# A planner that knows of the SBUF port which VectorE and GpSimd share

## The chip, the cores and the metric

The kernel runs on one core of a Trainium2 chip. The core has a matrix engine (TensorE, in the profile PE, with PEld for its weight loads), a vector engine (VectorE, DVE), an engine for activation functions (ScalarE, ACT), a general one (GpSimd, POOL) and a queue that issues DMAs (SyncE, SP). Each engine works through its own list of instructions in order and waits on semaphores for the others. The metric is device time in microseconds of one execution; shorter is better.

## What is computed

A two-layer backbone over 512 latent tokens and 256 context tokens of width 1024, all in float32. Cut to what matters:

```python
for i in range(DEPTH):                                  # 2 layers
    sh1, sc1, g1, sh2, sc2, g2 = split(silu(c) @ mod_w[i] + mod_b[i], 6)
    a = rmsnorm(h) * (1 + sc1) + sh1
    m = ab_mixer(a, ac) if i == 0 else hyena_mixer(a)   # ac: the context, modulated
    h = h + g1 * m
    u = rmsnorm(h) * (1 + sc2) + sh2
    h = h + g2 * ((silu(u @ w1) * (u @ w3)) @ w2)       # width 2816
return rmsnorm(h)
```

The first mixer runs four heads of gated DeltaNet (chunks of 64 tokens, a triangular solve per chunk, a scan in both directions) and four heads of gated linear attention. The second is a Hyena operator: a short convolution and two long convolutions, done here with DFT matrices, whose filters come from a small network of sines.

## The kernel before

The kernel is written once as a straight program, but its calls do not go to the chip directly. A `Recorder` stands in for the engines: every call becomes an `Op` with its engine, an estimated cost, its dependences and a section name, and `Recorder.schedule` then makes one order for all engines. `Recorder.issue` emits the instructions in that order, so each engine's list, and the list of DMAs on SyncE, is what the planner decided. All instructions therefore carry one line, 648, in the profile.

The planner is a list scheduler. It keeps a clock `free[e]` per engine. Again and again it takes the engine that can start first, and of the operations that are ready there by then it takes the one with the highest priority: the longest path of costs to the end, plus an offset. The offsets are the table `BOOST`: one number for a section, one for a section on one engine (`"f1@gpsimd"`), in nanoseconds of path. Sections are stages of the program: `vec`, `mlp`, `modc`, `in` (inputs and modulation), `f0` to `f3` (Hyena's filters), `g`, `n0` to `n3`, `p0` to `p3`, `i0`, `i2`, `s0` to `s3`, `l0`, `l1`, `h0` to `h3`, `z0` to `z7` (the first mixer), `m02` to `m04`, `mods` (more modulation), `out`, `fa`, `fa0` to `fa3` with `fa0o` to `fa3o` (first feed-forward layer), `dft`, `p0h` to `p3h`, `v0h` to `v3h`, `hy`, `hyout` (Hyena), `fb` and its kin (second feed-forward layer). Some parts raise their own priority with `urgent`.

The planner also models the bank of PSUM that each matmul's output takes, ScalarE's table loads, the landing of DMAs and TensorE's clock; where TensorE would idle long it puts in a matmul on a constant tile. SBUF addresses are fixed before the planner runs and do not depend on its order.

A float32 product is made of three products of rounded numbers: `split` writes a rounded copy on ScalarE (a CAST) and the rest of it with a VectorE subtraction of two SBUF tiles (`t<-t ... fp32r`). This pair precedes nearly every matmul, for weights and for activations. GpSimd gets elementwise work on SBUF tiles: additions and subtractions in `filter_chunk`, in `gdn_scan` a scaling of 128x128 tiles, in Hyena's `conv` and `group` differences and gate products, in the feed-forward layers the weight difference `S3` of each `unit`. No GpSimd call here reads PSUM; a good part of VectorE's work does (`t<-bank,t`).

Of the kernel before, what the change touches and what calls it, by code (L numbers as in the profile page):

```python
# [19 lines left out]
P = 128  # L20
# [12 lines left out]
BOOST = {"": 1200, "@gpsimd": 19800, "@vector": -113900, "c": -161700, "c@gpsimd": 173900, "c@sync": -82400,  # L33
         "dft": 21800, "dft@scalar": 56000, "dft@sync": 21800, "dft@vector": -318200, "end": 12900,
         "end@scalar": -111300, "end@sync": -75800, "end@tensor": 253300, "end@vector": 46500, "f0": -3200,
# [19 lines left out]
         "fb@scalar": 22200, "fb@tensor": -4600, "fb@vector": 7200, "ffn0": -123100, "ffn0@scalar": 54200,  # L55
# [5 lines left out]
         "h3@scalar": 117400, "h@sync": 7500, "h@tensor": -117000, "h@vector": -38300, "ht@scalar": 11900,  # L61
         "ht@tensor": 89700, "hy": -14100, "hy@scalar": 26800, "hy@sync": 111000, "hy@tensor": -100100,
         "hy@vector": -3900, "hyout": -1600, "hyout@scalar": -23500, "hyout@sync": -38900, "hyout@vector": -24700,
# [10 lines left out]
         "m15@tensor": 4100, "m15@vector": 55800, "mlp": 9500, "mlp@scalar": 51700, "mlp@sync": -11600,  # L74
         "mlp@tensor": 29000, "modc": 40000, "modc@tensor": -1400, "modc@vector": -2300, "mods": 148900,
         "mods@sync": 12100, "mods@tensor": 6000, "mods@vector": -1900, "n0": 1900, "n0@gpsimd": -6000,
# [3 lines left out]
         "out@scalar": -2900, "out@sync": 7000, "out@tensor": 177300, "p0": -22500, "p0@gpsimd": -483000,  # L80
# [15 lines left out]
         "vec": -17400, "vec@scalar": -72600, "vec@sync": -1400, "vec@tensor": 1000, "vec@vector": 10000,  # L96
# [131 lines left out]
class VTile:  # L228
    __slots__ = ("phys", "left", "slot", "bit", "anc")
# [3 lines left out]


class Op:
    __slots__ = ("eng", "calls", "cost", "deps", "succ", "vts", "prio", "path", "idx", "nd", "bytes", "start", "end", "ready", "sec", "tbl", "anc", "alias", "inst", "rows", "first", "last")


class EngineProxy:
# [19 lines left out]
class Recorder:  # L259
# [75 lines left out]
    def add(s, eng, name, a, k):  # L335
# [10 lines left out]
        op = None  # L346
# [2026 lines left out]
```

## Time and profile before

| | |
|---|---|
| three runs | 1673.51, 1678.25, 1680.84 us; median 1678.25 |
| the profiled execution | 1673.98 us, of which the span from first to last instruction is 1672.3 |
| TensorE busy | 1590.1 us (95%), 11356 matmuls |
| VectorE busy | 1248.1 us (75%), 2158 instructions |
| ScalarE busy | 791.1 us (47%) |
| GpSimd busy | 364.9 us (22%), 430 instructions |
| DMA | 201.25 MB, mean 120 GB/s |

Busy time is the time during which at least one instruction of the engine runs. An instruction that has started and is held up by something inside the chip counts as busy, so a long mean duration can hide a wait; the durations by shape are to be read beside the shares. A matmul's recorded end is modelled, so full busy time of TensorE is not its peak rate.

### The profile page before, as it was taken

Reading aid. Unit: us, or ns where it says so; the run is one execution under the profiler, and the core shown is the slowest. Engines: PE = TensorE matmul, PEld = TensorE weight load, DVE = VectorE, ACT = ScalarE, POOL = GpSimd, SP = SyncE. Lnnn points to the kernel's source line nnn. Section 1 sums busy time; section 2 is a strip of 40 time slices with the busy share of each in tenths; the row PEclk is TensorE's granted clock in tenths of the full one; section 3 lists DMA queues with packets and bytes.
Section 4 is the critical chain, followed back from the end, with each engine's and each line's share of the span. In section 5 each row is a group of like instructions: output and inputs, shape, how many; then the busy total and the mean of one; then the engine's idle time right before and its main releaser. Section 6 shows DMA issues by size and latency. Waiting matters only on the chain.

```text
span 1672.3 us, 29141 instructions
## 1 busy us (share of the span) xinstructions
PE 1590.1 (95%) x11356; PEld 1400.8 (84%) x11356; DVE 1248.1 (75%) x2158; ACT 791.1 (47%) x1503; POOL 364.9 (22%) x430
## 2 busy tenths in 40 slices
PE   6999889999999889999999999999999999999998
PEld 3687778778777579989989898888889898989898
DVE  4878985657375886968678688598896977868676
ACT  3556533642434444644536365343344653636353
POOL 0344653513232310101010100143440101011000
PEclk9999997998899889999999999999999999999999
DMA  8744332473266432243343354333432333333331
GB/s 284 208 146 152 108 110 68 160 234 112 75 203 211 130 114 64 82 108 90 88 125 95 109 155 134 97 108 92 133 92 76 102 89 101 99 104 98 106 96 56
DMA packets 257147, 201.25 MB, mean 120 GB/s; under 512 B 11281, under 2 KB 234447, under 8 KB 257008
## 3 DMA queue, kind: packets, MB, share of 16 engines
q1 hardware_dynamic: 257008, 199.39, 39.5%
q8 instruction: 89, 1.46, 0.4%
q14 instruction: 50, 0.41, 0.1%
HBM read 185.70 MB, written 13.66 MB: 119 GB/s over the span
## 4 chain that ended last, share of the span: by engine, by line
PE 64%; DVE 21%; ACT 5%; DMA 4%; issue 3%; POOL 3%; SPq 0%; DVEq 0%; POOLq 0%; ACTq 0%
PE bank L648 64%; DVE t L648 21%; ACT t L648 5%; POOL t L648 3%; DMA t<-in_ffn_w_dram 1%; DMA kscr<-t 0%; SPq L648 0%; DMA t<-in_mod_w_dram 0%; ACT L641 0%; DMA t<-in_dft_filt_dram 0%; DMA t<-in_hy_w_in_dram 0%; DMA t<-in_ctx_dram 0%; DMA t<-gscr 0%; DMA t<-in_hy_w_out_dram 0%; DMA t<-in_dft_fwd_dram 0%
## 5 line engine op out<-in xcount | busy, mean ns | idle before, releaser
L648 PE MATMUL bank<-t 128*128 128x256 f32 (+8 forms) x11356 | 1590.1, 316 | 76.2 <-DVE t L648 47.0
L648 PEld LDWEIGHTS bank<-t 128*128 128x128 f32 (+4 forms) x11356 | 1400.8, 183 | 265.3 <-DVE t L648 72.7
L648 DVE TENSOR_TENSOR t<-t 128x512 fp32r<-128x512 f32 (+11 forms) x1151 | 795.7, 728 | 229.3 <-ACT t L648 150.8
L648 ACT CAST t<-t 128x512 fp32r<-128x512 f32 (+4 forms) x651 | 421.6, 664 | 428.7 <-PE bank L648 203.7
L648 POOL TENSOR_TENSOR t<-t 128x256 f32<-128x256 f32 (+3 forms) x230 | 268.5, 1186 | 952.2 <-DMA t<-in_ffn_w_dram 507.8
L648 ACT ACTIVATE t<-t 128x256 f32<-128x256 f32 (+8 forms) x314 | 156.4, 530 | 151.7 <-DVE t L648 132.0
L648 DVE TENSOR_TENSOR t<-bank,t 128x256 f32<-128x256 f32 (+5 forms) x305 | 147.3, 511 | 63.3 <-PE bank L648 50.7
L648 DVE SCALAR_TENSOR_TENSOR t<-bank,t 128x511 f32<-128x511 f32 (+4 forms) x248 | 143.1, 592 | 52.4 <-PE bank L648 35.4
L648 ACT COPY t<-bank 128x256 f32<-128x256 f32 (+2 forms) x272 | 106.8, 408 | 122.7 <-PE bank L648 119.8
L648 ACT ACTIVATE t<-bank 128x256 f32<-128x256 f32 (+7 forms) x134 | 51.0, 389 | 114.3 <-PE bank L648 111.6
L648 ACT ACTIVATE t<-bank,t 128x512 f32<-128x512 f32 (+3 forms) x94 | 51.2, 557 | 57.5 <-PE bank L648 37.4
L648 POOL COPY t<-t 32x192 f32<-32x192 f32 (+3 forms) x96 | 41.7, 440 | 132.9 <-DVE t L648 112.8
L648 DVE SCALAR_TENSOR_TENSOR t<-t 128x256 f32<-128x256 f32 (+7 forms) x134 | 59.4, 494 | 4.3 <-ACT t L648 3.8
L648 DVE SCALAR_TENSOR_TENSOR t<-t,bank 64x128 f32<-64x128 f32 (+1 forms) x112 | 38.0, 345 | 32.1 <-PE bank L648 29.5
L648 DVE COPY t<-bank 128x256 f32<-128x256 f32 (+8 forms) x70 | 31.2, 456 | 24.9 <-PE bank L648 23.4
L648 POOL TENSOR_SCALAR t<-t 128x128 f32<-128x128 f32 x40 | 31.0, 781 | 64.7 <-PE bank L648 31.5
L641 ACT ACT_TABLE_LOAD x32 | 41.1, 1283 | 1.4 <-PEq L2360 0.8
L648 POOL MEMSET t<- 32x192 f32 (+10 forms) x47 | 18.3, 394 | 78.2 <-PE bank L648 58.9
L648 DVE TENSOR_SCALAR t<-t 128x256 f32<-128x256 f32 (+5 forms) x57 | 23.9, 440 | 3.3 <-ACT t L648 2.8
L648 DVE TENSOR_TENSOR_SCAN t<-t 64x768 f32<-64x768 f32 x8 | 14.0, 1750 | 0.2
L648 DVE STREAM_TRANSPOSE t<-t 128x1024 f32<-128x1024 f32 x6 | 10.4, 1755 | 0.3
L648 POOL TENSOR_SCALAR_AFFINE_SELECT t<-t 128x512 f32<-128x512 f32 (+1 forms) x11 | 6.6, 609 | 13.2 <-DVE t L648 13.2
(15 smaller groups left out, 33.6 us busy)
## 6 DMA issues: line engine op xcount, KB each, us to landing
t<-in_mod_w_dram SPq DMA_DIRECT2D x96, 512.0 KB, 4.0
t<-in_ffn_w_dram SPq DMA_DIRECT2D x88, 512.0 KB, 4.1
t<-in_ffn_w_dram SPq DMA_DIRECT2D x48, 384.0 KB, 3.6
t<-in_ab_w_in_dram SPq DMA_DIRECT2D x28, 512.0 KB
t<-in_hy_w_in_dram SPq DMA_DIRECT2D x24, 512.0 KB, 4.3
kscr<-t SPq DMA_DIRECT2D x72, 128.0 KB, 1.8
t<-kscr SPq DMA_DIRECT2D x24, 256.0 KB, 2.6
t<-in_ffn_w_dram SPq DMA_DIRECT2D x16, 256.0 KB, 2.9
```

Source lines behind the costliest of these rows:

```text
L641: s.nc.scalar.add_instruction(mybir.InstLoadActFuncSet(name=s.nc.get_next_instruction_name(), engine=mybir.EngineType.Activation, act_func ...
L648: r = getattr(getattr(s.nc, o.eng), name)(*[b(x) for x in a], **{n: b(x) for n, x in k.items()})
```

## The change

Every instruction stays on its engine. An `Op` gets a mark `lock`. A VectorE call sets it when more than one of its inputs is a wide SBUF tile, or when it is a `tensor_copy` or `tensor_scalar` with one such input and no PSUM operand. A GpSimd call sets it unless it is a `memset`. In the planner a marked operation of one of the two engines starts no earlier than the planned end of the last marked operation of the other one (`port`). The planned start decides the order. The offsets in `BOOST` for the sections that the program uses are replaced by others, most of them, on all engines (the old and new table have some 330 entries each; those shown are a sample).

```diff
--- before.py
+++ after.py
@@ -30,77 +30,76 @@
 CH = 64
 COLS = 52480
 CW = 256
-BOOST = {"": 1200, "@gpsimd": 19800, "@vector": -113900, "c": -161700, "c@gpsimd": 173900, "c@sync": -82400,
...
+BOOST = {"": -15600, "@gpsimd": -13200, "@vector": 1000, "c": 1100, "c@gpsimd": -8600, "c@sync": 4400, "dft": 4600,
+         "f0@sync": -8700, "f0@tensor": 65300, "f0@vector": 51100, "f1": -5300, "f1@gpsimd": -142800,
+         "fa2o@tensor": -2300, "fa2o@vector": 1800, "fa3": 600, "fa3@gpsimd": 393800, "fa3@scalar": -1500,
...
@@ -233,7 +232,7 @@
 
 
 class Op:
-    __slots__ = ("eng", "calls", "cost", "deps", "succ", "vts", "prio", "path", "idx", "nd", "bytes", "start", "end", "ready", "sec", "tbl", "anc", "alias", "inst", "rows", "first", "last")
+    __slots__ = ("eng", "calls", "cost", "deps", "succ", "vts", "prio", "path", "idx", "nd", "bytes", "start", "end", "ready", "sec", "tbl", "anc", "alias", "inst", "rows", "first", "last", "lock")
 
 
 class EngineProxy:
@@ -349,7 +348,7 @@
         if op is None:
             op = Op()
             op.eng, op.calls, op.cost, op.deps, op.succ, op.vts, op.prio, op.idx = eng, [], 0.0, set(), [], {}, s.boost + BOOST.get(f"{s.sec}@{eng}", 0.0), len(s.ops)
-            op.bytes, op.tbl, op.sec, op.alias, op.inst, op.rows, op.first, op.last = 0, None, s.sec, set(), None, P, None, None
+            op.bytes, op.tbl, op.sec, op.alias, op.inst, op.rows, op.first, op.last, op.lock = 0, None, s.sec, set(), None, P, None, None, False
             s.ops.append(op)
             if s.gr is not None:
                 s.gr[0] = op
@@ -438,6 +437,8 @@
             op.last = form
             op.cost += c
         elif eng == "vector":
+            sb = sum(1 for x in ins if not isinstance(x, View) and (len(x.shape) > 2 or x.shape[1] > 1))
+            op.lock = op.lock or sb > 1 or (sb == 1 and not ps and name in ("tensor_copy", "tensor_scalar"))
             if name == "reciprocal":
                 op.cost += n * 6.25 + 68
             elif name == "tensor_tensor_scan":
@@ -452,6 +453,7 @@
             op.cost += n * 0.8333 + (51 if ps else 93) + 51 * sc
             op.tbl = k.get("func") or next((x for x in a if isinstance(x, AF)), None)
         else:
+            op.lock = name not in ("memset",)
             if name == "tensor_copy":
                 op.cost += n * 1.25 + 130
             elif name in ("memset", "affine_select"):
@@ -523,6 +525,7 @@
                 heapq.heappush(pend[o.eng], (0.0, o.prio, o.idx))
         order = []
         curtbl = form = None
+        port = {"vector": 0.0, "gpsimd": 0.0}
         low, done, placed = 0, [False] * n, 0
         left = n
         while left:
@@ -572,6 +575,9 @@
                 if g is not None and g != curtbl:
                     c += 1283
                     curtbl = g
+            if o.lock:
+                t = max(t, port["gpsimd" if e == "vector" else "vector"])
+                port[e] = t + c
             o.start, o.end = t, t + c
             if e == "tensor":
                 if form is not None and o.first != form:
@@ -627,7 +633,7 @@
         v.slot = bank
         x = s.idle
         o.eng, o.calls, o.vts, o.alias, o.tbl, o.idx = "tensor", [("matmul", (View(v)[:, :P],), dict(lhsT=x, rhs=x, start=True, stop=True))], {v: True}, (), None, -1
-        o.cost, o.start, o.inst, o.sec, o.bytes, o.deps = P * 4 / 2.4, start, None, "warm", 0, ()
+        o.cost, o.start, o.inst, o.sec, o.bytes, o.deps, o.lock = P * 4 / 2.4, start, None, "warm", 0, (), False
         return o
 
     idle = None
```

## Rows read from the trace of the kernel before

**Rows 1.** Busy time by stretch: start:end length, engines' busy us (count), clock, DMA share, GB/s
```profile
0.00:600.00 600.00, 545.17 (x4138) 433.82 (x4139) 419.38 (x870) 280.17 (x541) 215.68 (x294) 0.93 0.49 156
...
720.00:987.00 267.00, 267.00 (x1848) 249.00 (x1847) 197.85 (x284) 126.44 (x244) 24.41 (x16) 1.00 0.36 102
987.00:1334.00 347.00, 334.75 (x2174) 300.38 (x2173) 282.24 (x453) 157.12 (x273) 85.87 (x96) 1.00 0.38 113
1334.00:1638.00 304.00, 303.96 (x2128) 285.06 (x2129) 226.20 (x329) 147.06 (x284) 25.39 (x17) 0.99 0.34 96
...
sum 1672.30, PE 1590.10 PEld 1400.76 DVE 1248.08 ACT 791.06 POOL 364.93; mean PE 265.02 PEld 233.46 DVE 208.01 ACT 131.84 POOL 60.82
```

**Rows 2.** The chain that ended last, shares of the span by engine
```profile
PE 64%; DVE 21%; ACT 5%; DMA 4%; issue 3%; POOL 3%; SPq 0%; DVEq 0%; POOLq 0%; ACTq 0%
```

**Rows 3.** A stretch where GpSimd hardly works, VectorE's groups of 987 to 1050
```profile
1000.00:1050.00 50.00, 49.16 (x330) 44.44 (x329) 41.31 (x87) 25.82 (x50) 0.67 (x3) 1.00 0.45 139
...
L648 DVE TENSOR_TENSOR t<-t 128x512 fp32r<-128x512 f32 x16 | 10.6, 686 | 1.5 <-ACT t L648 1.3
L648 DVE TENSOR_TENSOR t<-t 128x256 f32<-128x256 f32 x20 | 7.7, 417 | 0.7 <-ACT t L648 0.6
...
L648 DVE TENSOR_TENSOR t<-t 128x1024 fp32r<-128x1024 f32 x6 | 7.2, 1220 | 4.8 <-ACT t L648 4.8
```

**Rows 4.** VectorE's groups by shape, whole kernel: xcount | busy us, mean ns | idle before
```profile
L648 DVE TENSOR_TENSOR t<-t 128x512 fp32r<-128x512 f32 x428 | 311.2, 750 | 63.4 <-ACT t L648 48.3 <-PE bank L648 13.1
L648 DVE TENSOR_TENSOR t<-t 128x512 f32<-128x512 f32 x224 | 172.7, 786 | 50.8 <-ACT t L648 33.7 <-DMA t<-in_ffn_w_dram 13.3 <-POOL t L648 3.1
L648 DVE TENSOR_TENSOR t<-t 128x1024 fp32r<-128x1024 f32 x76 | 101.4, 1343 | 39.9 <-ACT t L648 35.5 <-PE bank L648 4.2
...
L648 DVE TENSOR_TENSOR t<-t 128x256 fp32r<-128x256 f32 x81 | 40.8, 526 | 9.4 <-ACT t L648 9.0
```

**Rows 5.** GpSimd's groups by shape, whole kernel
```profile
L648 POOL TENSOR_TENSOR t<-t 128x512 f32<-128x512 f32 x82 | 122.0, 1492 | 711.4 <-DMA t<-in_ffn_w_dram 507.8 <-DVE t L648 152.0 <-ACT t L648 44.0
L648 POOL TENSOR_TENSOR t<-t 128x256 f32<-128x256 f32 x128 | 108.3, 874 | 173.7 <-DVE t L648 170.1 <-ACT t L648 3.2
```

**Rows 6.** Timeline, two moments at which GpSimd works alone: start, us, what
```profile
146.54 0.73 POOL L648 TENSOR_TENSOR t<-t 128x256 f32<-128x256 f32 x1
...
1265.57 2.52 POOL L648 TENSOR_TENSOR t<-t 128x512 f32<-128x512 f32 x2 [13.11 <-DVE t L648]
```

**Rows 7.** VectorE and GpSimd by shape in the stretch 720 to 987
```profile
L648 DVE TENSOR_TENSOR t<-t 128x512 fp32r<-128x512 f32 x136 | 99.4, 748 | 25.5 <-ACT t L648 19.6 <-PE bank L648 5.4
L648 DVE TENSOR_TENSOR t<-t 128x512 f32<-128x512 f32 x65 | 52.1, 811 | 17.1 <-ACT t L648 9.2 <-DMA t<-in_ffn_w_dram 7.7
...
L648 POOL TENSOR_TENSOR t<-t 128x512 f32<-128x512 f32 x16 | 24.4, 1533 | 227.6 <-DMA t<-in_ffn_w_dram 208.0 <-DVE t L648 19.5
```

**Rows 8.** Timeline, 706 to 713
```profile
707.15 3.08 DVE L648 TENSOR_TENSOR t<-t 128x512 f32<-128x512 f32 x5
...
708.01 3.37 POOL L648 TENSOR_TENSOR t<-t 128x512 f32<-128x512 f32 x1 [9.82 <-DMA t<-in_ffn_w_dram]
...
712.63 0.62 PE L648 MATMUL bank<-t 128*128 128x256 f32 x3 [0.92 <-ACT t L648]
```

**Rows 9.** Timeline, 1084 to 1092
```profile
1086.62 3.24 POOL L648 TENSOR_TENSOR t<-t 128x1024 f32<-128x1024 f32 x1 [9.20 <-DVE t L648]
1089.89 2.62 DVE L648 TENSOR_TENSOR t<-t 128x512 f32<-128x512 f32 x4 [2.28 <-POOL t L648]
```

**Rows 10.** VectorE by shape, 1050 to 1250
```profile
L648 DVE TENSOR_TENSOR t<-bank,t 128x512 f32<-128x512 f32 x72 | 44.9, 682 | 19.7 <-PE bank L648 19.2
...
L648 DVE TENSOR_TENSOR t<-t 128x512 fp32r<-128x512 f32 x34 | 28.3, 870 | 0.1
```

**Rows 11.** Table loads of ScalarE, and the load queue's longest wait
```profile
L641 ACT ACT_TABLE_LOAD x32 | 41.1, 1283 | 1.4 <-PEq L2360 0.8
...
SPq L648 <- DVE t L648: 972.8, 249, 27.3
```

More of the change, by code (lines that the diff above doesn't have):

```diff
@@ L32 @@
 CW = 256
-BOOST = {"": 1200, "@gpsimd": 19800, "@vector": -113900, "c": -161700, "c@gpsimd": 173900, "c@sync": -82400,
-         "dft": 21800, "dft@scalar": 56000, "dft@sync": 21800, "dft@vector": -318200, "end": 12900,
-         "end@scalar": -111300, "end@sync": -75800, "end@tensor": 253300, "end@vector": 46500, "f0": -3200,
[19 rows of a table removed]
-         "fb@scalar": 22200, "fb@tensor": -4600, "fb@vector": 7200, "ffn0": -123100, "ffn0@scalar": 54200,
[5 rows of a table removed]
-         "h3@scalar": 117400, "h@sync": 7500, "h@tensor": -117000, "h@vector": -38300, "ht@scalar": 11900,
-         "ht@tensor": 89700, "hy": -14100, "hy@scalar": 26800, "hy@sync": 111000, "hy@tensor": -100100,
-         "hy@vector": -3900, "hyout": -1600, "hyout@scalar": -23500, "hyout@sync": -38900, "hyout@vector": -24700,
[7 rows of a table removed]
+BOOST = {"": -15600, "@gpsimd": -13200, "@vector": 1000, "c": 1100, "c@gpsimd": -8600, "c@sync": 4400, "dft": 4600,
[12 rows of a table added]
+         "fa3o@sync": 9400, "fa@scalar": 17200, "fa@sync": -2800, "fa@tensor": -5200, "fa@vector": -70000,
[10 rows of a table added]
+         "g": 119000, "g@gpsimd": 17300, "g@scalar": 15200, "g@sync": -17900, "g@tensor": 1200, "g@vector": 4200,
[3 rows of a table added]
+         "h@vector": 142900, "ht@scalar": 11900, "ht@tensor": 89700, "hy": -13700, "hy@scalar": -104400,
+         "hy@sync": 163800, "hy@vector": -14800, "hyout": -800, "hyout@scalar": 93900, "hyout@sync": 8100,
[7 rows of a table added]
          "m10@tensor": -9600, "m10@vector": -8000, "m11": -27500, "m11@sync": 87500, "m11@vector": 25000,
@@ L73 @@
          "m13@sync": -9100, "m13@vector": -4100, "m14": 31100, "m14@sync": -162900, "m15": 5700, "m15@sync": 49200,
-         "m15@tensor": 4100, "m15@vector": 55800, "mlp": 9500, "mlp@scalar": 51700, "mlp@sync": -11600,
-         "mlp@tensor": 29000, "modc": 40000, "modc@tensor": -1400, "modc@vector": -2300, "mods": 148900,
-         "mods@sync": 12100, "mods@tensor": 6000, "mods@vector": -1900, "n0": 1900, "n0@gpsimd": -6000,
[3 rows of a table removed]
-         "out@scalar": -2900, "out@sync": 7000, "out@tensor": 177300, "p0": -22500, "p0@gpsimd": -483000,
[15 rows of a table removed]
-         "vec": -17400, "vec@scalar": -72600, "vec@sync": -1400, "vec@tensor": 1000, "vec@vector": 10000,
[7 rows of a table removed]
+         "m15@tensor": 4100, "m15@vector": 55800, "mlp": 112500, "mlp@scalar": 35300, "mlp@sync": -10700,
+         "mlp@tensor": -7300, "mlp@vector": 80500, "modc": -3000, "modc@tensor": -9900, "modc@vector": 40200,
[4 rows of a table added]
+         "n3@sync": 73400, "n3@vector": -70300, "out": -8500, "out@scalar": -34000, "out@sync": -400,
[15 rows of a table added]
+         "v3h@vector": 5400, "vec": -23700, "vec@tensor": -59800, "vec@vector": 111900, "z0@gpsimd": 17500,
[7 rows of a table added]
 XACT = (0, 1, 2, 4, 5, 6)
```

112 rows, old and new, of the table BOOST are left out of this document.

## The prediction

> **What bounds the kernel now.** I read the stretches first. In the two feed-forward stretches, 720 to 987 and 1334 to 1638 us, TensorE is busy 267.00 of 267 us and 303.96 of 304 us [rows 1]: 571 us in which a better order of VectorE or GpSimd can give nothing back and a worse one can only take. In the first 600 us (modulation, filters, the recurrent heads) it is busy 545.17 us at a mean granted clock of 0.93 of full speed, so 55 us are open gaps there; from 987 to 1334 (Hyena) the gaps are 12 us [rows 1].
>
> Next the chain of work that ended last: 64% of it is TensorE, 21% VectorE, 3% GpSimd [rows 2]. That is 351 us (0.21 x 1672.3) of VectorE and 50 us of GpSimd which decide the time. Outside the two feed-forward stretches VectorE is busy 1248.08 - 197.85 - 226.20 = 824 us and GpSimd 364.93 - 24.41 - 25.39 = 315 us [rows 1], so there 43% of VectorE's busy time lies on the chain and 16% of GpSimd's.
>
> Then the groups by shape, to see whether the two engines hold each other up at all. From 1000 to 1050 us GpSimd works 0.67 us; in the stretch that holds it, a VectorE subtraction of two SBUF tiles takes 686 ns for 512 columns, 1220 for 1024 and 417 for 256 [rows 3]. Over the whole kernel the same shapes average 750 and 786, 1343 and 526 ns [rows 4]. A VectorE instruction of 512 columns that reads a bank instead of a second tile takes 682 ns in the Hyena stretch, where GpSimd is busy, and its neighbours with two tiles take 870 ns there [rows 10]. So the reader is to see a real conflict: it is between VectorE with two SBUF inputs and GpSimd, and the planner of before knows nothing of it.
>
> What it adds up to: VectorE 428 x 64 ns + 224 x 100 + 76 x 123 + 81 x 109 (this one against the 417 of the plain shape of equal columns) = 27.4 + 22.4 + 9.3 + 8.8 = 68 us [rows 3, 4]. In a feed-forward stretch it is 136 x 62 + 65 x 125 = 16.6 us [rows 7], and 33 for both if the second is like the first; 35 us are left outside. GpSimd takes 1260 ns for 512 columns and 730 for 256 when left alone [rows 6] and 1492 and 874 on average [rows 5]: 82 x 232 + 128 x 144 = 37 us, of which 16 x 273 ns = 4.4 us lie in one feed-forward stretch [rows 7], 29 us outside both. The smaller groups are left out.
>
> **The change part by part.** *The flag and the two port clocks in the planner* add no instruction and take none away. They change the start that the planner writes down for a flagged instruction, hence the order in which all five queues are filled. What the order can win is bounded by the stall on the chain. Lower bound: stalls spread evenly over on- and off-chain work, 35 x 0.43 + 29 x 0.16 = 20 us. Upper bound: all of it on the chain, 35 + 29 = 64 us. I take the middle, 42 us: the rows show both kinds, a GpSimd product between two VectorE instructions of one dependence, for which VectorE stands 2.28 us [rows 9], and the stalls of the feed-forward stretches that TensorE hides entirely [rows 1, 7].
>
> Of these 42 us I count half as won, 21 us. A planner that knows of the port doesn't make the port wider: one of the two engines still waits unless something else can stand beside GpSimd. Such work exists: 72 VectorE instructions on banks, 44.9 us, in the Hyena stretch alone [rows 10], against 85.87 us of GpSimd from 987 to 1334 [rows 1]. But the multiply of 3.24 us between VectorE's sums and its next ones [rows 9] has its neighbours fixed by data. If that cover fails everywhere the gain is nothing; if it holds everywhere it is the 42, at most the 64.
>
> The flag is also set where rows don't ask for it: a masked copy from a bank counts its own output as an input. Such over-reservations cost the chip nothing by themselves, only order.
>
> *The offsets* move instructions within and between stages on all queues. They issue the same work: the same matmuls apart from the planner's warm-up matmuls, the same loads. Two things can change in number or place. Activation-table loads, 32 of 1283 ns, 41.1 us [rows 11], come from alternating functions in ScalarE's order; four more or fewer would be 5 us of an engine that is busy only 280.17 of the first 600 us [rows 1], so I cost them at nothing; if its slack there were gone it would be the 5 us. And the load queue: SyncE's queue waits for VectorE 972.8 us in 249 waits [rows 11], that is, loads go out when VectorE frees a buffer. A VectorE instruction that the plan holds back for the port holds back the load queued behind it, and all later loads on that one queue; the matmuls that need that weight wait next. From 720 to 1334 DMA's share is under 0.4 [rows 1], so there is room for this, and I cost it at nothing; without that cover each such step would cost what VectorE is held, at most one GpSimd operation of 1.26 us [rows 6].
>
> One rule of the Trainium skill is weighed here, and no number above needs it. At 708.01 a GpSimd subtraction starts while VectorE has begun a run of five at 707.15 that lasts 3.08 us, to 710.23; GpSimd's ends at 711.38, after 3.37 us [rows 8]. Five in 3.08 us is 0.62 each, so the second of the run ended near 708.38; GpSimd waited through three more. The Trainium skill, "SBUF — State Buffer", section "Who interferes with whom", says that whichever engine issues first holds the shared pair for the whole instruction and the other blocks, which is how the new planner's clocks work. By that rule the subtraction would have run from 708.38 to 709.64, 1.74 us before it did; the trace agrees with the blocking and differs in who comes next. By the rule alone the forecast would be that all the chain's 42 us can be planned round, 1632 us; by the row it is less, and the last rival follows.
>
> **The sum.** The profiled execution took 1673.98 us, a span of 1672.3 and 1.7 around it; the median of the three runs shown is 1678.25, 4.3 more. 1674 - 21 = 1653 us.
>
> **The rivals.**
> *It gives more.* The whole 42 us of chain stall goes, up to the 64 of the upper bound: 1632 to 1610, middle 1621. For it: 55 us of open TensorE gaps in the first 600 us [rows 1], so there is something to fill. Against: the fixed neighbours of [rows 9].
> *The planner does on paper what the chip did anyway.* The blocked time becomes planned waiting and the order that comes out is no better: 1674, within 6 us. For it: 571 us are TensorE's own [rows 1], and 84% of GpSimd's work is off the chain.
> *GpSimd comes late (the other side).* The plan gives GpSimd the port after one VectorE instruction; the chip lets VectorE's run go on, as at 708.01, and the product comes up to 1.74 us after its planned time; TensorE stood 0.92 us there [rows 8]. By the 16% above, 34 of the 210 two-tile operations of GpSimd [rows 5] lie on the chain. At half of 1.74, 0.87 us each, that is 30 us: 1704 if the forecast's gain fails, 1683 if it comes whole, 1693 between. It decides, over 0.5% slower than the median, from 15 such operations without the gain (12.6 / 0.87). Against it: the planner of before has the same late products and pays for them in the 1674 already.
>
> **How the numbers follow.** Forecast 0.45 (own range 1638 to 1668), more 0.17, no change 0.21, late GpSimd 0.17. 0.5%, 8.4 us, is about what a measurement here tells from no change: faster means under 1669.9, slower over 1686.6. Faster: 0.45 + 0.17 and a little of the third, 0.04, is 0.66. Slower: most of the last, 0.14. The same: 0.20. The range drops the lower half of "more" (0.08) and the upper part of the last (0.11): 1618 to 1690.
>
> **What would show it.** Right: VectorE's mean for 512 columns of two tiles falls from 750 and 786 towards 686, GpSimd's 1492 and 874 towards 1260 and 730, and the first 600 us' work ends some 15 us earlier, the rest of the gain in Hyena; the feed-forward stretches keep their length. Wrong: the means fall and the span does not (the waiting was only moved, second rival); means stay and the span falls (the offsets did it, not the port); GpSimd operations of 3 us and gaps of TensorE in the feed-forward stretches (the last). A feed-forward stretch longer than 270 or 307 us would alone undo the forecast.

## The result and the profile after

The changed kernel takes 1655.04 us, median of four runs (1653.48 to 1659.42), against 1676.57 for before in the same comparison: ratio 0.9874, 95% interval 0.9844 to 0.9904, 21.5 us less. The forecast was 1653.

The profiled execution is the longest of the four (1659.42, span 1657.7). Its stretches, to be read beside [rows 1] (stretch, length, busy us of PE, PEld, DVE, ACT and POOL with counts, clock, DMA share, GB/s), the chain's shares beside [rows 2], TensorE's longest wait (first of before, then of after: us in total, times, longest), and the table loads beside [rows 11]:

```profile
0.00:600.00 600.00, 562.65 (x4275) 454.63 (x4276) 416.91 (x882) 273.62 (x538) 212.16 (x295) 0.93 0.49 156
600.00:720.00 120.00, 117.52 (x913) 112.30 (x913) 98.48 (x167) 69.43 (x140) 8.75 (x6) 1.00 0.32 90
720.00:987.00 267.00, 267.00 (x1848) 249.01 (x1847) 196.61 (x283) 128.04 (x245) 24.82 (x16) 1.00 0.37 106
987.00:1334.00 347.00, 344.97 (x2303) 314.78 (x2303) 290.35 (x464) 161.32 (x281) 86.74 (x97) 1.00 0.37 110
```

```profile
PE 76%; DVE 11%; DMA 4%; ACT 4%; issue 2%; POOL 2%; SPq 1%; DVEq 0%; POOLq 0%; ACTq 0%
```

```profile
PE bank L648 <- DVE t L648: 47.0, 59, 2.9
```

```profile
PE bank L654 <- DVE t L654: 19.8, 41, 1.3
```

```profile
L647 ACT ACT_TABLE_LOAD x26 | 33.4, 1283 | 1.2 <-PEq L2366 0.8
```

VectorE's share of the chain has fallen from 21% to 11%, 351 to 182 us, and TensorE's has risen from 64% to 76%. TensorE's open gaps in the first 600 us went from 55 to 37 us, from 987 to 1334 from 12 to 2. Part of that is the planner's warm-up matmuls, which count as busy and of which after has more: where they are not issued (below), the gaps are 62 us in the order of before and 52 in that of after, and from 987 to 1334 15 and 24.

Now the durations by shape, to be read beside [rows 4] and [rows 5] (count | busy us, mean ns | idle before, what ended it):

```profile
L654 DVE TENSOR_TENSOR t<-t 128x512 fp32r<-128x512 f32 x428 | 318.5, 766 | 68.8 <-ACT t L654 51.9 <-PE bank L654 14.5
L654 DVE TENSOR_TENSOR t<-t 128x512 f32<-128x512 f32 x224 | 164.9, 751 | 45.9 <-ACT t L654 27.9 <-DMA t<-in_ffn_w_dram 9.9 <-POOL t L654 7.7
L654 DVE TENSOR_TENSOR t<-t 128x1024 fp32r<-128x1024 f32 x76 | 100.1, 1321 | 37.4 <-ACT t L654 34.2 <-PE bank L654 2.9
...
L654 DVE TENSOR_TENSOR t<-t 128x256 fp32r<-128x256 f32 x81 | 40.4, 513 | 12.9 <-ACT t L654 12.4 <-DMA kscr<-t 0.2 <-PE bank L654 0.2
...
L654 POOL TENSOR_TENSOR t<-t 128x512 f32<-128x512 f32 x82 | 116.8, 1429 | 732.5 <-DMA t<-in_ffn_w_dram 471.6 <-DVE t L654 164.1 <-PE bank L654 48.3
L654 POOL TENSOR_TENSOR t<-t 128x256 f32<-128x256 f32 x128 | 112.0, 905 | 174.5 <-DVE t L654 167.1 <-ACT t L654 4.0 <-DMA kscr<-t 3.0
```

They have hardly moved. The prediction's own sum over these rows gives 428 x 80 ns + 224 x 65 + 76 x 101 + 81 x 96 = 64 us of stall for VectorE where it gave 68, and 82 x 169 + 128 x 175 = 36 us for GpSimd where it gave 37. The two engines hold each other up as much as before; a smaller part of it lies where it sets the end.

Where the time came from, by the two long pieces of TensorE's work on the chain (start, length, instructions), first of before, then of after:

```profile
719.56 267.54 PE bank L648 x1848
1334.04 303.56 PE bank L648 x2123
```

```profile
712.79 267.54 PE bank L654 x1848
...
1297.31 325.66 PE bank L654 x2338
```

The first feed-forward stretch starts 6.8 us sooner and is as long to the hundredth. The second piece ends at 1637.60 in before and 1622.97 in after, 14.6 us sooner, so 7.9 us more were won between, in Hyena and the norm behind it. These 14.6 us are the whole difference of the two profiled executions; the other 7 of the 21.5 us by the medians are in no trace shown here.

### The profile page after: what moved, and what is told of

It is laid out like the page before. It is cut to its first block, busy times and chain, and to the rows that moved or that the text cites. A ratio compares the mean times of both kernels' runs of the same rounds, so it can differ in the third digit from the quotient of the medians.

```text
span 1657.7 us, 29630 instructions
## 1 busy us (share of the span) xinstructions
PE 1609.4 (97%) x11596; PEld 1428.5 (86%) x11596; DVE 1237.7 (75%) x2158; ACT 784.4 (47%) x1497; POOL 356.3 (21%) x430
## 4 chain that ended last, share of the span: by engine, by line
PE 76%; DVE 11%; DMA 4%; ACT 4%; issue 2%; POOL 2%; SPq 1%; DVEq 0%; POOLq 0%; ACTq 0%
PE bank L654 76%; DVE t L654 11%; ACT t L654 4%; POOL t L654 2%; DMA t<-in_mod_w_dram 1%; DMA kscr<-t 1%; SPq L654 1%; DMA t<-in_ab_w_in_dram 1%; DMA t<-in_hy_w_in_dram 0%; DMA t<-in_hy_filt_out_dram 0%; DMA t<-in_dft_inv_dram 0%; DMA t<-in_ffn_w_dram 0%; ACT L647 0%; DMA t<-in_window_dram 0%; DMA t<-in_dft_fwd_dram 0%
## 5 line engine op out<-in xcount | busy, mean ns | idle before, releaser
L654 PE MATMUL bank<-t 128*128 128x256 f32 (+6 forms) x11596 | 1609.4, 315 | 42.3 <-DVE t L654 19.8
L654 PEld LDWEIGHTS bank<-t 128*128 128x128 f32 (+3 forms) x11596 | 1428.5, 183 | 223.0 <-issue 40.5
L654 DVE TENSOR_TENSOR t<-t 128x512 fp32r<-128x512 f32 (+13 forms) x1151 | 785.4, 719 | 230.3 <-ACT t L654 148.8
L654 ACT CAST t<-t 128x512 fp32r<-128x512 f32 (+3 forms) x651 | 420.8, 665 | 452.9 <-PE bank L654 225.1
L654 POOL TENSOR_TENSOR t<-t 128x256 f32<-128x256 f32 (+3 forms) x230 | 263.9, 1167 | 968.4 <-DMA t<-in_ffn_w_dram 471.6
L654 ACT ACTIVATE t<-t 128x256 f32<-128x256 f32 (+7 forms) x314 | 156.1, 529 | 127.6 <-DVE t L654 109.4
L654 DVE TENSOR_TENSOR t<-bank,t 128x256 f32<-128x256 f32 (+4 forms) x305 | 147.3, 513 | 63.3 <-PE bank L654 47.0
L654 ACT COPY t<-bank 128x256 f32<-128x256 f32 (+3 forms) x272 | 107.7, 409 | 135.3 <-PE bank L654 130.2
L654 DVE COPY t<-bank 128x256 f32<-128x256 f32 (+7 forms) x70 | 31.2, 458 | 33.6 <-PE bank L654 32.2
L654 POOL MEMSET t<- 32x192 f32 (+10 forms) x47 | 18.3, 393 | 103.9 <-DVE t L654 59.4
L654 DVE TENSOR_SCALAR t<-bank,t 64x512 f32<-64x512 f32 (+1 forms) x5 | 3.9, 780 | 8.3 <-DMA t<-in_hy_freq_dram 5.0
```

The source lines that it names most:

```text
L654: r = getattr(getattr(s.nc, o.eng), name)(*[b(x) for x in a], **{n: b(x) for n, x in k.items()})
```

## The experiments

Three theories stood at the start. A: knowing the port takes stalls off the chain. B: the new offsets are simply better ones. C: planner and offsets work only as a pair that was searched together.

**The planner with the port, the offsets of before.**

```diff
 (after.py)
-BOOST = {"": -15600, "@gpsimd": -13200, "@vector": 1000, ...
+BOOST = {"": 1200, "@gpsimd": 19800, "@vector": -113900, ...
```

> The planner with the port, the offsets of before. Theory A (knowing the port is what took the stalls off the chain): at least half of the 21.5 us gain, 1655 to 1666. Theory B (the new offsets alone order the work better): no gain, 1671 to 1685. Theory C (offsets and planner only work as a pair, searched together): no gain or a loss, 1671 to 1700, and the kernel with the new offsets alone shows none either.

1689.91 us, ratio 1.0093 (1.0070 to 1.0115): slower than before. As a whole the flag alone gains nothing: the time of theory A is missed, that of B too, and C's range holds. The first feed-forward piece starts at 746.40 (rows below), 27 us later than in before.

```profile
746.40 268.86 PE bank L655 x1859
```

```profile
PE bank L655 <- DVE t L655: 23.3, 30, 2.9
```

TensorE's waits for VectorE went down all the same, to 23.3 us, half of the 47.0 of before. And from the end of the first feed-forward piece to the end of the span this kernel takes 1692.3 - 746.40 - 268.86 = 677.0 us, like after (1657.7 - 712.79 - 267.54 = 677.4), where before takes 1672.3 - 719.56 - 267.54 = 685.2 (one profile each; the three orders planned with the port at the end of this section, where the offsets are shaken and searched further, take 680.2, 678.2 and 675.3). So the flag alone brings the 8 us behind that layer, and what it loses is lost ahead of it. The planner put three times as many warm-ups into this order as into that of before (11798 matmul records against 11356; 11140 are left in either order when no warm-up is issued, and each has two, so 329 against 108). How much of the loss is theirs was not tried.

**The new offsets, the planner without the port.**

```diff
 (after.py)
-            if o.lock:
-                t = max(t, port["gpsimd" if e == "vector" else "vector"])
-                port[e] = t + c
```

> The planner without the port, the new offsets. Theory A: nothing is gained, 1670 to 1690, and VectorE and GpSimd stall on the chain as before. Theory B: the whole gain, 1650 to 1660. Theory C: no gain or a loss, 1671 to 1700.

1687.59 us, ratio 1.0077 (1.0053 to 1.0100): slower too, so B falls; the ranges of A and C both hold. The chain still has 16% of VectorE, TensorE waits for VectorE as long as in before, and the first feed-forward piece starts at 735.45; what follows it takes 1689.1 - 735.45 - 267.54 = 686.1 us, near the 685.2 of before:

```profile
PE 69%; DVE 16%; DMA 5%; ACT 4%; POOL 2%; issue 2%; SPq 1%; DVEq 0%; POOLq 0%; ACTq 0%
```

```profile
PE bank L647 <- DVE t L647: 47.2, 54, 6.7
```

```profile
735.45 267.54 PE bank L647 x1848
```

**Each order without the conflict.** In `issue`, nearly every GpSimd call that reads SBUF becomes memsets of its output with the waits of the call (`fill` issues as many as take about as long as the call does alone); the arithmetic of these calls is left out.

```diff
+                if o.eng == "gpsimd" and name != "memset" and o.idx > 6:
+                    r, last = s.fill(o, name, a)
...
-                    for d in sorted(o.alias):
+                    for d in sorted(set(o.alias) | ({d for d in o.deps if d in s.filled} if o.idx not in s.filled else set(o.deps))):
```

> The order of before; nearly every GpSimd instruction that reads SBUF is replaced by memsets of the same output that take about as long as it does when left alone and wait for the same work, so that its arithmetic is left out and nothing is left to contend for the port on reads. Theory A: the stalls on the chain go, 42 us (20 to 64), so 1612 to 1657, and VectorE's mean for 512 columns of two tiles is near 686 ns everywhere. Theories B and C: the chain loses little by the port, under 15 us, 1661 to 1677.

> The order of after with the same replacement, its arithmetic left out likewise. Theory A: what is left on the chain is small, it falls by less than half of what the order of before falls by, to 1635 to 1655. Theories B and C: it falls by as much as the order of before does, whatever that is.

The order of before: 1626.76 us, ratio 0.9706 (0.9686 to 0.9726), 46.6 us less. The order of after: 1650.84 us, ratio 0.9861 (0.9847 to 0.9876), 4 us less than after, which the intervals do not tell from nothing (some 2 us by the ratios, 0.9861 and 0.9874, each against before in its own comparison). Both times lie where A put them and not where B and C did. Groups by shape and the two pieces of TensorE on the chain of the first, then of the second:

```profile
L651 DVE TENSOR_TENSOR t<-t 128x512 fp32r<-128x512 f32 x428 | 285.4, 687 | 93.7 <-ACT t L651 70.9 <-PE bank L651 21.0
L651 DVE TENSOR_TENSOR t<-t 128x512 f32<-128x512 f32 x224 | 149.9, 685 | 50.8 <-ACT t L651 35.9 <-DMA t<-in_ffn_w_dram 11.5 <-POOL t L685 2.6
...
L685 POOL MEMSET t<- 128x512 f32 x172 | 90.4, 526 | 724.5 <-DMA t<-in_ffn_w_dram 555.6 <-DVE t L651 112.4 <-ACT t L651 44.2
...
L685 POOL MEMSET t<- 128x156 f32 x46 | 10.5, 229 | 2.6
```

```profile
689.07 267.54 PE bank L651 x1848
...
1290.75 300.66 PE bank L651 x2123
```

```profile
L657 DVE TENSOR_TENSOR t<-t 128x512 fp32r<-128x512 f32 x428 | 285.4, 687 | 99.3 <-ACT t L657 75.0 <-PE bank L657 20.8
```

```profile
707.89 267.54 PE bank L657 x1848
...
1291.21 325.65 PE bank L657 x2338
```

The reader is to see three things. First, VectorE is back at the 686 ns of [rows 3], so the contention is gone, though GpSimd is not quicker in its largest group: two memsets of 526 ns and one of 229 stand for a subtraction of 1260 [rows 6]. (Over all groups it is busy 307.4 us, where 364.9 less the 37 of the prediction's sum gives 328: the smaller ones had stalls too, or their memsets are some 20 us too short.) This also agrees with the Trainium skill, "SBUF — State Buffer", section "Who interferes with whom", that a VectorE instruction with two SBUF inputs contends with a GpSimd instruction that reads SBUF and not with one that only writes it. Second, the contention cost the order of before 46.6 us, 30.5 of them ahead of the first feed-forward layer (719.56 to 689.07), and costs the order of after hardly anything measurable. What the stall takes from the clock is in the 46.6: the mean granted clock is 0.978 to 0.983 in the four executions without contention and 0.971 to 0.976 in those of before, at most some 12 us between the medians (0.007 x 1673). Third, without contention the order of before is the better one by 24 us: it gets to the first feed-forward layer at 689.07, the other at 707.89, so 19 of the 24 lie there. It is not the clock: one of the executions of the order of after without contention had a mean granted clock of 0.981, as high as the other order, and took 1650.47 us. Theory A is right about the place, and wrong in that the knowledge is free: 46.6 us of stall on the chain became 4.2, and the order is 24.1 us (1650.84 - 1626.76) less tight: 46.6 - 4.2 - 24.1 = 18.3, which is the 21.5 but for the 3.2 by which the median of before differs between the two comparisons (1676.57 and 1673.32). That the 24 us are the price of avoiding the stall is likely, not shown: the offsets and the number of warm-ups differ as well, a loose order hides a stall by itself, and no run takes the contention out of the two orders in which one thing alone was changed.

**The warm-up matmuls.** After has 240 matmul records more than before (11596 against 11356), the planner's warm-ups, two records each. They are not issued here:

```diff
         for o in order:
+            if o.sec == "warm":
+                continue
```

> The order of after, the planner's warm-up matmuls not issued (they compute nothing that is used). Theory W (the warm-ups, of which the new order has twice as many, hold TensorE where the chip leaves it no gap: matmuls of 128 columns on 128 rows take 20.2 us from 1240 to 1345 against 10.9 before): faster, 1635 to 1650. Theory G (they only fill gaps in which TensorE waits for VectorE anyway, and keep its clock up): no change or slower, 1653 to 1670.

> The order of before, the warm-ups not issued. Theory W: there are half as many, and the chip's gaps of before are wide there, so it falls by less than 9 us, 1664 to 1673. Theory G: no change or slower, 1673 to 1690.

> The order of after, GpSimd replaced by memsets as in the earlier run of that order (its arithmetic is left out), and no warm-ups. Theory W: the 4 us which that order gained without contention were so few because the warm-ups held TensorE; without them it comes down to 1625 to 1642. Theory G: it stays at 1645 to 1655, and the order of after is really less tight than that of before.

After without them: 1671.60 us, ratio 0.9990 (0.9972 to 1.0009), 16.6 us lost by the medians, some 19 by the ratios (0.9990 and 0.9874). Before without them: 1680.21, ratio 1.0039 (1.0019 to 1.0060), some 6 us lost. The order of after without contention and without them: 1657.83, ratio 0.9901 (0.9875 to 0.9927), 7 us more than with them. Theory W falls three times; the warm-ups are worth having, most in the order of after, and there a little more than G allowed: its ranges are passed by 1.6 and 2.8 us. Two stretches of after (the row of 600 to 720 stands with the result), then after without them, last two stretches of before without them:

```profile
1230.00:1280.00 50.00, 49.79 (x377) 47.37 (x376) 37.96 (x59) 22.13 (x41) 10.42 (x10) 1.00 0.26 75
1280.00:1330.00 50.00, 49.84 (x418) 49.19 (x418) 46.94 (x82) 33.46 (x69) 5.94 (x4) 1.00 0.34 93
```

```profile
0.00:600.00 600.00, 548.22 (x4128) 440.51 (x4128) 421.89 (x884) 275.07 (x540) 212.95 (x295) 0.92 0.49 156
600.00:720.00 120.00, 105.27 (x769) 100.68 (x770) 94.88 (x161) 66.06 (x133) 9.11 (x6) 0.94 0.32 89
...
1230.00:1280.00 50.00, 42.76 (x281) 39.65 (x282) 36.36 (x51) 17.98 (x29) 11.00 (x11) 0.93 0.25 75
1280.00:1330.00 50.00, 36.54 (x285) 35.12 (x284) 45.81 (x84) 34.31 (x73) 5.86 (x4) 0.90 0.31 85
```

```profile
987.00:1334.00 347.00, 323.48 (x2063) 292.28 (x2062) 284.90 (x455) 159.07 (x274) 85.18 (x96) 0.97 0.37 111
```

```profile
0.00:600.00 600.00, 537.62 (x4088) 426.28 (x4088) 415.94 (x864) 279.11 (x541) 213.19 (x293) 0.94 0.49 156
...
987.00:1334.00 347.00, 332.37 (x2114) 297.54 (x2112) 278.31 (x449) 157.10 (x276) 83.92 (x95) 0.98 0.37 112
```

Without them TensorE works, in the order of after, 42.76 and 36.54 of 50 us at a mean granted clock of 0.93 and 0.90 of 2.4 GHz; with them it is at 1.00. At most 120 x 0.06 + 50 x 0.07 + 50 x 0.10 = 15.7 us hang on the clock of these three stretches, if TensorE's work set the pace all through them.

**More warm-ups.** Each is issued twice, in either order:

```diff
-            for name, a, k in o.calls:
+            for name, a, k in o.calls * (2 if o.sec == "warm" else 1):
```

> The order of before, each warm-up matmul issued twice, about as many as the order of after has. Theory V (some 10 of the 21.5 us are no matter of the port: the new planner sees wider gaps of TensorE, puts twice the warm-ups in, and these are worth 16.6 us in the new order and 5.8 in the old): it gets part of this, 1662 to 1669. Theory P (warm-ups help only in the gaps of the order that they were planned for): no change or slower, 1671 to 1685.

> The order of after, each warm-up matmul issued twice. Theory V (more warm-ups, more clock): 1645 to 1655. Theory P (those that are there fill the gaps; more take TensorE's time, 0.22 us each for the two passes, 20 us from 1240 to 1345 alone): slower, 1665 to 1690.

Before: 1679.54, ratio 1.0033 (1.0006 to 1.0060). After: 1688.06, ratio 1.0090 (1.0067 to 1.0113). Theory V, that the count makes the gain, falls. They pay in the gaps that the planner sized them for, and past that they take TensorE's time: in the order of after, matmuls of 128 columns from 1240 to 1345 take 35.0 us in this run and 20.2 in after. The rows, of after and of after with them twice:

```profile
L654 PE MATMUL bank<-t 128*128 128x128 f32 x178 | 20.2, 275 | 0.0
```

```profile
L654 PE MATMUL bank<-t 128*128 128x128 f32 x311 | 35.0, 275 | 0.0
```

**The offsets shaken.**

```diff
+for _i, _k in enumerate(sorted(BOOST)):
+    BOOST[_k] += (_i * 7919 % 4001) - 2000
```

> After, with every offset moved by a fixed step of at most 2 us of path, the port in the planner as it is. Theory A (knowing the port gives the gain): within 8 us of after, 1647 to 1663. Theory C (planner and offsets are fitted to each other by search): most of the gain is lost, 1665 to 1700.

1665.20, ratio 0.9955 (0.9934 to 0.9976): 9.2 us less than before in the same comparison (1674.37), so more than half of the 21.5 us is gone by moving offsets of up to 393800 by at most 2000. It lies 2 us outside A's range and at the edge of C's. The chain shows no return of the stalls:

```profile
PE 79%; DVE 8%; DMA 5%; ACT 3%; POOL 2%; issue 1%; SPq 1%; DVEq 0%; ACTq 0%; POOLq 0%
```

So VectorE's share of the chain stays small under other offsets too, as long as the planner knows the port (with the offsets of before TensorE's wait for VectorE was halved likewise), and the offsets decide how tight the rest is.

**The search carried on.** Two further walks over the offsets against the planner with the port; in each, some 380 of the 420 entries that one table or the other has differ from after's (a table has some 360, not the 330 said with the change).

```diff
-BOOST = {"": -15600, "@gpsimd": -13200, "@vector": 1000, ...
+BOOST = {...}
```

> After, with the offsets searched further against the planner that knows the port (a random walk over them that keeps what shortens the planned end). Theory F (with the port in it the planner is true enough that what it gains on paper the chip gains in good part): 1638 to 1649. Theory L (further search only fits the planner's own errors): 1651 to 1670.

> The same from another walk, whose planned end is some 4 us later than that of the first. Theory F: 1641 to 1652, and not before the first. Theory L: 1651 to 1670, in no order.

1654.71, ratio 0.9876 (0.9855 to 0.9897), and 1659.76, ratio 0.9909 (0.9886 to 0.9933). Theory F falls, L's range holds: of what the planner gains on paper from here (how much is not on record) the chip gives nothing that the intervals show. No version that does all the arithmetic beat the changed kernel by more than the noise.

## Why the prediction was right, point by point

**The bound.** TensorE alone sets both feed-forward stretches: the first piece is 267.54 us before, after, with the new offsets alone and without contention. Right.

**The stall on the chain, 42 us (20 to 64).** The write-only run of before's order measures it: 46.6 us, with what the stall takes from the clock in it. Right, and the middle was nearer than either end.

**Half of it won, 21 us.** The sum came out, its reason did not. The step said that half stays because one of the two engines still waits. In the run one of the two does still wait, as long as before (64 and 36 us against 68 and 37), but no longer on the chain: there at most 4.2 us stay, so nearly all was taken off; and 24 us came back as an order that is less tight, 19 of them ahead of the first feed-forward layer, for which the forecast counted nothing. Two errors of nearly one size cancel: that 1653 came so near 1655 is luck. Behind the first feed-forward layer the port is enough (677.0 us with the old offsets, 677.4 with the new, 685.2 and 686.1 without it); ahead of it each alone loses (746.40 and 735.45 against 719.56) and only the pair gains (712.79). Which instructions make the order less tight was not tried and stays open.

**Costed at nothing: the warm-ups.** The step left them out of the count of what moves. There are 120 more of them, and they are worth 16.6 us or more in the new order and about 6 in the old; without any, the two orders are only 8.6 us apart (1680.21 and 1671.60). Some 13 of the 21.5 us thus need them. It is not made by their number, as the runs with twice as many show, and the runs do not split the 21.5 us into a share of the port and a share of the clock, since the planner sizes one by the other.

**Costed at nothing: table loads and the load queue.** 26 loads instead of 32, 7.7 us of ScalarE. Neither was tried by itself.

**The rule and its rival.** By the rule of the Trainium skill, "SBUF — State Buffer", section "Who interferes with whom", alone all the stall could be planned round, which the prediction put at 1632 us. The stall could be, the time could not. The late GpSimd of the last rival did not come: TensorE waits for VectorE 19.8 us in all, where it was 47.0, for ScalarE, over which the late product of [rows 8] reached it, 9.0, where it was 19.8, and GpSimd's 512 columns are shorter on average than before, 1429 against 1492 (its 256 columns are longer, 905 against 874). That the planner's turn-taking is not the chip's cost nothing that these runs tell from noise.

**The second rival**, waiting moved from the chip to the paper with no gain, is nearest to what the planner with the old offsets did, though its 1689.91 lies beyond the 6 us around 1674 that the rival allowed.

**What was to show it.** Wrong: means towards 686 and 1260 ns. They stayed at 766, 751 and 1429. By the prediction's own sign (means stay, the span falls) the offsets did it, not the port; the run with the new offsets alone says otherwise. I had taken the mean of a group for a sign of the chain; the share of the chain is the sign. Right: the feed-forward stretches keep their length. Half right: 15 us ahead of the first of them and the rest in Hyena; it was 6.8 and 7.9.

## What to carry to other kernels

A sum over inflated durations bounds a contention; what it costs is only what lies on the chain, and that can go to nearly nothing while the durations stay. To measure it, keep the order and the waits and take the contention out, here by writing where GpSimd read: the difference of the two orders then splits into what the stall cost and what the new order costs without it. Where a planner's model and its tuned offsets change together, run each alone before crediting either: here each alone was slower than what it replaced. And look where it was slower: behind the first feed-forward layer the port alone was worth as much as the pair.

## What the runs showed of the hardware that was not expected

Matmuls whose results nothing reads were worth 16.6 us by the medians in one order: without them the granted clock was 0.94 from 600 to 720 us and 0.93 and 0.90 from 1230 to 1330, in stretches where TensorE was busy 105.27 of 120, 42.76 of 50 and 36.54 of 50 us, and with them 1.00. Twice as many cost the same order 33 us by the medians (1688.06 against 1655.04).
